# A two-stream diffusion layer on one core: VectorE's sums for a gate moved one transfer later and tied behind a subtraction

## The chip, the cores and the metric

The kernel runs on one core of a Trainium2 chip. The time is the device time of one execution in microseconds (us), the median of three runs. A profile is one execution more, with its own time; the trace is of that execution, and its span reaches from the first to the last instruction of the core.

## What is computed

One layer of a diffusion trunk is applied to two streams of 128 tokens with 2048 features: a context stream and a latent stream, which share all weights. Cut to what matters here:

```python
def adaln_params(cvec, w_ada_l, b_ada_l):
    mod = jax.nn.silu(cvec) @ w_ada_l + b_ada_l          # one vector per stream, 6 x 2048
    return jnp.split(mod[..., None, :], 6, axis=-1)      # sh1, sc1, g1, sh2, sc2, g2

h = modulate(rmsnorm(x, norm_mix_w), sh1, sc1) @ w_in    # 2048 x 8192
...                                                      # gated recurrence, short convolution, attention
x = x + g1 * (mixed @ w_out)                             # 2048 x 2048
h = modulate(rmsnorm(x, norm_ffn_w), sh2, sc2)
x = x + g2 * ((silu(h @ w_gate) * (h @ w_up)) @ w_down)  # hidden size 5632
```

The change touches the two gates, `g1` and `g2`: products of a vector per stream with a column block of `w_ada`, where the weights are read once and used for two vectors.

## The kernel before

**The stream of weights.** Every matrix is read in tiles of 512 rows by 512 columns (1 MB). `split` (line 238; `feature_mm`, line 289, does the same for weights that are held transposed) issues the tile's transfer on SyncE's queue, and then for each half of it ScalarE rounds the weights to the fp32r type (`hi`, line 253) and VectorE subtracts what was rounded from the weights (`lo`, line 254; line 299 in `feature_mm`). TensorE multiplies with both: per half tile eight matmuls with `hi` and four with `lo`, each of 512 columns, over two token streams (`products`, line 267). `hi` and `lo` have three buffers each, the raw tile four. In the last tiles of a matrix (`last_mm`) both halves have buffers of their own, and one token stream ends before the other.

**The modulation's weights.** There are 24 column blocks (chunks of 512 columns) of `w_ada`. The first eight are made ahead. Of the others, `LATER_T` (and chunk 20, in the pause behind `w_out`) go through TensorE (`later_pe`), and the seven chunks of `LATER_V`, 8 to 11 of `g1` and 21 to 23 of `g2`, through VectorE (`later_dve`, line 401): a chunk comes in eight parts, and each part is a GpSimd copy (line 411, which lets the transfer begin only when a recent tile is written), a transfer of 512 KB on GpSimd's queue (line 412) into one of two buffers `araw`, and four sums (line 415, `scalar_tensor_tensor`, 128x512 each) that add weights times the conditioning vector into `aacc`, of which there is one buffer. With the eighth part `later_gate` is started (lines 364 to 381): rounding on ScalarE (373), a subtraction (374), two matmuls that add over the partitions (379), and a copy out of PSUM (380), for each token stream.

**What sets the order.** The work is written down in an order made by hand. After each tile `behind` is called: it lets every started generator go on by one step (`pump`), and `ada_step` adds the phase's pace to two queues and takes parts from them when enough has come together. A part of a VectorE chunk costs 0.5; the pace of that queue is `PACE_V` = 0.19, 0.39, 0.08, 0.35 in the phases 0 to 3, which are the last round over the first seven column blocks of `w_in`, the other nine, `w_out`, and the feed-forward part without its first chunk. `gate(c)` (line 437) is called before a gate is used and takes whatever of it is still missing. The program is then put into an order for each engine by a planner: it plays the program through with a model of the durations and gives each engine, among the instructions that are ready in that model, the one with the best priority, which is its place in the program. Splits are raised by 600 places (`SPLIT_AHEAD`). On the chip each engine follows the order so made.

Of the kernel before, what the change touches and what calls it, by code (L numbers as in the profile page):

```python
# [10 lines left out]
F32 = mybir.dt.float32  # L11
# [4 lines left out]
ALU = mybir.AluOpType  # L16
# [76 lines left out]
def trunk(ctx: ExitStack, tc: tile.TileContext, a: dict):  # L93
    nc = tc.nc
    pool = ctx.enter_context(tc.tile_pool(name="sb", bufs=1))
    psum = ctx.enter_context(tc.tile_pool(name="ps", bufs=1, space=PSUM))
    uid = [0]
    ahead = [0]

    def sb(shape, tag, bufs, dt=F32):  # L100
        uid[0] += 1
        return pool.tile(shape, dt, tag=tag, name=f"{tag}_{uid[0]}", bufs=bufs)

    def const(shape, name, dt=F32):
        return pool.tile(shape, dt, tag=name, name=name, bufs=1)

    def u4(shape=(P, 2, CH)):
        return sb(list(shape), "u4", U4_BUFS)

    def u8(shape=(P, 2, 2, 4, P), dt=F32):  # L110
        return sb(list(shape), "u8", U8_BUFS, dt)

    def st(shape=(P, CH), dt=F32):
        return sb(list(shape), "st", ST_BUFS, dt)

    def aux(shape=(P, CH)):
        uid[0] += 1
        return psum.tile(list(shape), F32, tag="aux", name=f"aux_{uid[0]}", bufs=3)

    def accs():  # L120
        r = []
        for s in range(2):
            uid[0] += 1
            r.append(psum.tile([P, CH], F32, tag="acc", name=f"acc_{uid[0]}", bufs=4))
        return r
# [25 lines left out]
    cs = const([P, 16, 2], "cs")  # L151
# [76 lines left out]
    def spawn(gen):  # L228
        if next(gen, active) is not active:
            active.append(gen)  # L230

    def pump():
        for gen in list(active):
            if next(gen, active) is active:
                active.remove(gen)


    def split(src, apart=False):

        n = src.shape[1]  # L240
        with tc.high_priority(offset=ahead[0]):
            raw = sb([P, 4, CH], "raw", RAW_BUFS)
            nc.sync.dma_start(raw[:, 0:n], src)
            parts = []
            if apart:
                his, los = u8((P, 4, CH), F32R), u8((P, 4, CH), F32R)
            for j in range(n // 2):
                if apart:
                    hi, lo = his[:, 2 * j:2 * j + 2], los[:, 2 * j:2 * j + 2]
                else:  # L250
                    hi = sb([P, 2, CH], "hi", HL_BUFS, F32R)
                    lo = sb([P, 2, CH], "lo", HL_BUFS, F32R)
                nc.scalar.activation(hi, raw[:, 2 * j:2 * j + 2], AF.Copy)  # L253
                nc.vector.tensor_tensor(lo, raw[:, 2 * j:2 * j + 2], hi.bitcast(F32), op=ALU.subtract)  # L254
                parts.append((hi, lo))
        return parts

# [12 lines left out]
    def split_mm(src, acc, lhs, first, last, k0=0):  # L270

        parts = split(src)
        n = src.shape[1]
        for k in range(0, n, 2):
            products([(s, acc[s]) for s in range(2)], (k, k + 1), lhs, k0, parts, first and k == 0, last and k == n - 2)

    def last_mm(steps, acc, phase):

        tiles = []
        for src, lhs in steps:  # L280
            tiles.append((split(src, True), lhs))
            behind(phase)
        for s in range(2):
            for t, (parts, lhs) in enumerate(tiles):
                for k in (0, 2):
                    products([(s, acc[s])], (k, k + 1), lhs, 0, parts, False, t == len(tiles) - 1 and k == 2)
            yield s

    def feature_mm(src, rhs, accs2, first, last):

        with tc.high_priority(offset=ahead[0]):
            raw = sb([P, 8, 256], "raw", RAW_BUFS)
            nc.sync.dma_start(raw, src)
            parts = []
            for j in range(2):
                hi = sb([P, 4, 256], "hi", HL_BUFS, F32R)
                lo = sb([P, 4, 256], "lo", HL_BUFS, F32R)
                nc.scalar.activation(hi, raw[:, 4 * j:4 * j + 4], AF.Copy)  # L298
                nc.vector.tensor_tensor(lo, raw[:, 4 * j:4 * j + 4], hi.bitcast(F32), op=ALU.subtract)  # L299
                parts.append((hi, lo))  # L300
        for k in range(8):
            hi, lo = parts[k // 4]
            x = rhs(k)
            for b in range(2):
                ws = slice(b * P, (b + 1) * P)
                one = accs2[b][:, 0:256].rearrange("p (s t) -> p s t", s=2)
                for i, (w, y) in enumerate(((hi, x[0]), (hi, x[1]), (lo, x[0]))):
                    nc.tensor.matmul(one, lhsT=w[:, k % 4, ws], rhs=y, start=first and k == 0 and i == 0,  # L308
                                     stop=last and k == 7 and i == 2)
# [54 lines left out]
    def later_gate(c, parts, pe):  # L364

        yield
        yield
        g = u4()
        hl = None
        for s in range(2):  # L370
            if hl is None or not pe:
                hl = [st(dt=F32R), st(dt=F32R)]
                nc.scalar.activation(hl[0], parts[s], AF.Copy)
                nc.vector.tensor_tensor(hl[1], parts[s], hl[0].bitcast(F32), op=ALU.subtract)
                yield
                yield
            ps = aux()
            for i in range(2):
                nc.tensor.matmul(ps, lhsT=selb[:, s, :] if pe else ones, rhs=hl[i], start=i == 0, stop=i == 1)  # L379
            nc.scalar.activation(g[:, s, :], ps, AF.Copy)  # L380
        gates[c] = g
# [19 lines left out]
    def later_dve(c, part, box):  # L401

        if part == 0:
            box["acc"] = sb([P, 2, CH], "aacc", 1)
            nc.gpsimd.tensor_copy(box["acc"][:, :, 0:1], S["late"][:, :, 0:1])  # L405
            nc.gpsimd.memset(box["acc"], 0.0)
            for s in range(2):
                nc.gpsimd.dma_start(box["acc"][0:1, s, :], a["b_ada"][0:1, c * CH:(c + 1) * CH])
        acc = box["acc"]
        raw = sb([P, 2, CH], "araw", 2)  # L410
        nc.gpsimd.tensor_copy(raw[:, :, 0:1], S["late"][:, :, 0:1])  # L411
        nc.gpsimd.dma_start(raw, a["w_ada2"][c - 8, part // 2, :, 2 * (part % 2):2 * (part % 2) + 2, :])  # L412
        for k in range(2):
            for s in range(2):
                nc.vector.scalar_tensor_tensor(acc[:, s, :], raw[:, k, :], cs[:, 2 * part + k, s:s + 1], acc[:, s, :],  # L415
                                               op0=ALU.mult, op1=ALU.add)
        if part == 7:
            spawn(later_gate(c, [acc[:, 0, :], acc[:, 1, :]], False))

    queues = []  # L420
    boxes = {}
# [7 lines left out]
    def ada_step(phase):  # L429
        for queue, amount in zip(queues, (PACE_T[phase], PACE_V[phase])):  # L430
            queue[2] += amount
            while queue[0] and queue[2] >= queue[1] - 1e-6:
                queue[2] -= queue[1]
                fn, c, part, box = queue[0].pop(0)
                fn(c, part, box)

    def gate(c):
        while c not in gates:
            pump()
            for queue, _, _ in queues:  # L440
                if any(item[1] == c for item in queue):
                    fn, *args = queue.pop(0)
                    fn(*args)
        return gates[c]

    def behind(phase=None):

        pump()
        if phase is not None:
            ada_step(phase)  # L450
# [416 lines left out]
    part = {}  # L867
    for ri, (k0, nk) in enumerate(ROUNDS):
# [4 lines left out]
        for i, name in enumerate(ORDER[:START]):  # L873
            acc = accs()
# [15 lines left out]
    for name in ORDER[START:]:  # L890
        if name in FM:
            for half in range(2):
                acc = accs()
                for q in range(2):
                    feature_mm(a["w_infm"][2 * FM.index(name) + half, q],
                               lambda k: tuple(hT[2 * q + k // 4][:, :, x, k % 4, :] for x in range(2)), acc, q == 0, q == 1)
                    behind(1)
                for b in range(2):
                    consume_fm(name, 2 * half + b, acc[b][:, 0:256].rearrange("p (s t) -> p s t", s=2))
            continue  # L900
        acc = accs()
        for q in range(4):
            split_mm(w_in(q, name), acc, hT[q], q == 0, q == 3)
            behind(1)
        t = u4()
        for s in range(2):
            nc.scalar.activation(t[:, s, :], acc[s], AF.Copy)
        consume(name, t)
# [4 lines left out]
    for n in range(4):  # L913
        acc = accs()
# [28 lines left out]
    while queues[0][0] or active:  # L943
        ada_step(4)
        pump()
# [53 lines left out]
    for gi, grp in enumerate(groups):  # L999
# [6 lines left out]
        for n in range(4):  # L1006
            acc = accs()
# [113 lines left out]
```

## Time and profile before

| | us |
|---|---|
| median of three runs (1380.97, 1381.04, 1384.13) | 1381.04 |
| the profiled execution, its own time | 1374.68 |
| its span | 1372.9 |
| TensorE busy | 1338.6 |
| VectorE busy | 872.9 |
| ScalarE busy | 627.4 |
| GpSimd busy | 132.6 |

A TensorE that is busy is not one at its peak, since matmuls are pipelined and their ends are modelled. The distance from the start of one matmul to the start of the next tells more. Times of day below are counted from the start of the span.

### The profile page before, as it was taken

Reading aid. Unit: us, or ns where it says so; the run is one execution under the profiler, and the core shown is the slowest. Engines: PE = TensorE matmul, PEld = TensorE weight load, DVE = VectorE, ACT = ScalarE, POOL = GpSimd, SP = SyncE. Lnnn points to the kernel's source line nnn. Section 1 sums busy time; section 2 is a strip of 40 time slices with the busy share of each in tenths; the row PEclk is TensorE's granted clock in tenths of the full one; section 3 lists DMA queues with packets and bytes.
Section 4 is the critical chain, followed back from the end, with each engine's and each line's share of the span. In section 5 each row is a group of like instructions: output and inputs, shape, how many; then the busy total and the mean of one; then the engine's idle time right before and its main releaser. Section 6 shows DMA issues by size and latency. Waiting matters only on the chain. (4 is left out here: it accounts for less than half of the span.)

```text
span 1372.9 us, 19781 instructions
## 1 busy us (share of the span) xinstructions
PE 1338.6 (97%) x7936; PEld 1078.0 (79%) x7936; DVE 872.9 (64%) x1102; ACT 627.4 (46%) x839; POOL 132.6 (10%) x201
## 2 busy tenths in 40 slices
PE   5999999999999999999999999999999999999996
PEld 3667777797798897778788888888888888888885
DVE  3355558986977687477944888655555554455564
ACT  4433447655465443446444444444334444444442
POOL 0100001131222221001200222000000000000000
PEclk9999999999999999999999999999999999999998
DMA  8898976875787889865765677555555555555551
GB/s 349 304 357 305 343 296 220 306 289 200 290 303 254 312 313 357 311 262 192 268 227 187 219 271 245 214 184 189 203 201 207 190 192 197 184 184 186 204 193 62
DMA packets 54381, 335.39 MB, mean 244 GB/s; under 512 B 7249, under 2 KB 7313, under 8 KB 19217
## 3 DMA queue, kind: packets, MB, share of 16 engines
q1 hardware_dynamic: 42768, 296.79, 59.0%
q0 software_dynamic: 10944, 36.29, 7.6%
q8 instruction: 62, 1.02, 0.3%
q10 hardware_dynamic: 576, 1.05, 0.2%
q14 instruction: 31, 0.25, 0.0%
HBM read 330.43 MB, written 3.67 MB: 243 GB/s over the span
## 5 line engine op out<-in xcount | busy, mean ns | idle before, releaser
L267 PE MATMUL acc<-hi,u 128*128 128x512 f32 x2944 | 741.2, 393 | 2.0 <-ACT u L488 1.1
L254 DVE TENSOR_TENSOR lo<-raw,hi 128x1024 fp32r<-128x1024 f32 x368 | 448.6, 1223 | 346.5 <-ACT hi L253 339.2
L267 PEld LDWEIGHTS acc<-hi,u 128*128 128x128 f32 x2944 | 548.7, 188 | 138.1 <-issue 10.4
L253 ACT ACTIVATE hi<-raw 128x1024 fp32r<-128x1024 f32 x368 | 388.8, 1060 | 544.2 <-PE acc L267 426.7
L267 PE MATMUL acc<-lo,u 128*128 128x512 f32 x1472 | 397.1, 390 | 1.8 <-DVE lo L254 1.7
L267 PEld LDWEIGHTS acc<-lo,u 128*128 128x128 f32 x1472 | 275.5, 188 | 63.0 <-DVE lo L254 3.7
L415 DVE SCALAR_TENSOR_TENSOR aacc<-araw,cs,aacc 128x512 f32<-128x512 f32 x224 | 159.0, 746 | 42.9 <-DMA araw<-w_ada 38.8
L308 PE MATMUL acc<-u,hi 128*128 128x256 f32 x768 | 142.2, 286 | 0.0
L308 PEld LDWEIGHTS acc<-u,hi 128*128 128x128 f32 x768 | 119.2, 191 | 9.7 <-issue 5.0
L308 PE MATMUL acc<-u,lo 128*128 128x256 f32 x384 | 108.3, 286 | 0.0
L332 PE MATMUL ada<-raw,cst 128*32 128x256 f32 (+1 forms) x784 | 83.7, 484 | 11.3 <-DMA raw<-w_ada 11.3
L298 ACT ACTIVATE hi<-raw 128x1024 fp32r<-128x1024 f32 x48 | 50.9, 1059 | 63.7 <-PE acc L308 34.5
L308 PEld LDWEIGHTS acc<-u,lo 128*128 128x128 f32 x384 | 72.8, 191 | 5.0 <-issue 4.2
L411 POOL COPY araw<-u 128x2 f32<-128x2 f32 x56 | 51.4, 920 | 257.7 <-DVE aacc L415 195.6
L299 DVE TENSOR_TENSOR lo<-raw,hi 128x1024 fp32r<-128x1024 f32 x48 | 58.2, 1218 | 15.3 <-ACT hi L298 12.0
L332 PEld LDWEIGHTS ada<-raw,cst 128*32 128x32 f32 x784 | 23.8, 114 | 38.0 <-issue 27.7
L882 DVE TENSOR_TENSOR u<-u,acc 128x512 f32<-128x512 f32 x56 | 35.9, 682 | 25.0 <-PE acc L267 24.9
L412 POOL DMA_DIRECT2D araw<-w_ada x56 | 30.0, 536 | 15.0 <-POOL araw L411 14.4
L405 POOL COPY aacc<-u 128x2 f32<-128x2 f32 x7 | 3.2, 453 | 266.6 <-DVE u L882 163.6
L484 ACT ACTIVATE st<-aux,sh,sc 128x128 f32<-128x128 f32 x48 | 18.1, 455 | 12.8 <-DVE sc L353 10.6
L267 PE MATMUL acc<-u,u 128*128 128x512 f32 x96 | 22.1, 389 | 0.0
L267 PEld LDWEIGHTS acc<-u,u 128*128 128x128 f32 x96 | 18.0, 188 | 3.7
(218 smaller groups left out, 627.0 us busy)
## 6 DMA issues: line engine op xcount, KB each, us to landing
raw<-w_ada SPq DMA_DIRECT2D x66, 1024.0 KB, 7.1
raw<-w_gate SPq DMA_DIRECT2D x44, 1024.0 KB, 4.8
raw<-w_up SPq DMA_DIRECT2D x44, 1024.0 KB, 4.8
raw<-w_down SPq DMA_DIRECT2D x44, 1024.0 KB, 4.8
raw<-w_in SPq DMA_DIRECT2D x33, 1024.0 KB, 6.8
araw<-w_ada POOLq DMA_DIRECT2D x56, 512.0 KB, 5.9
raw<-w_infm SPq DMA_DIRECT2D x24, 1024.0 KB, 5.6
raw<-w_out SPq DMA_DIRECT2D x16, 1024.0 KB, 7.2
```

What stands on the lines that cost most here:

```text
L253: nc.scalar.activation(hi, raw[:, 2 * j:2 * j + 2], AF.Copy)
L254: nc.vector.tensor_tensor(lo, raw[:, 2 * j:2 * j + 2], hi.bitcast(F32), op=ALU.subtract)
L267: nc.tensor.matmul(acc, lhsT=lhs[:, s, x, k0 + k, :], rhs=w[:, k % 2, :], start=first and k == ks[0] and w is hi and x == 0, stop=last and ...
L298: nc.scalar.activation(hi, raw[:, 4 * j:4 * j + 4], AF.Copy)
L299: nc.vector.tensor_tensor(lo, raw[:, 4 * j:4 * j + 4], hi.bitcast(F32), op=ALU.subtract)
L308: nc.tensor.matmul(one, lhsT=w[:, k % 4, ws], rhs=y, start=first and k == 0 and i == 0, stop=last and k == 7 and i == 2)
L332: nc.tensor.matmul(box["acc"][32 * k:32 * k + 32, 0:cols.stop - cols.start], lhsT=cst[:, 4 * part + k, 2 - row:34 - row], rhs=raw[k // 2][ ...
L411: nc.gpsimd.tensor_copy(raw[:, :, 0:1], S["late"][:, :, 0:1])
L412: nc.gpsimd.dma_start(raw, a["w_ada2"][c - 8, part // 2, :, 2 * (part % 2):2 * (part % 2) + 2, :])
L415: nc.vector.scalar_tensor_tensor(acc[:, s, :], raw[:, k, :], cs[:, 2 * part + k, s:s + 1], acc[:, s, :], op0=ALU.mult, op1=ALU.add)
L484: nc.scalar.activation(h[:, s, j, :], ps[:, s, j, :], AF.Identity, bias=bias, scale=scale)
L882: nc.vector.tensor_tensor(part[name][:, s, :], part[name][:, s, :], acc[s], op=ALU.add)
```

## The change

The four sums of a part are no longer written down with the part's own transfer. They are put into a list, `waiting`, and written down by `flush`, which the next part calls right after its own transfer (and `gate` in its loop, and `ada_step` when the queue is empty). While they are written down, `issue_after` gives each of them an edge to the newest `lo` subtraction of the stream that has been written down by then: VectorE's order must have them behind it. The edge is one of order on the engine and no wait on a semaphore. With the eighth part `later_gate` is started from the same place.

```diff
                 nc.scalar.activation(hi, raw[:, 2 * j:2 * j + 2], AF.Copy)
-                nc.vector.tensor_tensor(lo, raw[:, 2 * j:2 * j + 2], hi.bitcast(F32), op=ALU.subtract)
+                newest[0] = nc.vector.tensor_tensor(lo, raw[:, 2 * j:2 * j + 2], hi.bitcast(F32), op=ALU.subtract)
...
         nc.gpsimd.dma_start(raw, a["w_ada2"][c - 8, part // 2, :, 2 * (part % 2):2 * (part % 2) + 2, :])
-        for k in range(2):
-            for s in range(2):
-                nc.vector.scalar_tensor_tensor(acc[:, s, :], raw[:, k, :], cs[:, 2 * part + k, s:s + 1], acc[:, s, :],
-                                               op0=ALU.mult, op1=ALU.add)
-        if part == 7:
-            spawn(later_gate(c, [acc[:, 0, :], acc[:, 1, :]], False))
+        def sums():
+            with tc.issue_after(newest[0].ins):
+                for k in range(2):
+                    for s in range(2):
+                        nc.vector.scalar_tensor_tensor(acc[:, s, :], raw[:, k, :], cs[:, 2 * part + k, s:s + 1],
+                                                       acc[:, s, :], op0=ALU.mult, op1=ALU.add)
+            if part == 7:
+                spawn(later_gate(c, [acc[:, 0, :], acc[:, 1, :]], False))
+
+        flush()
+        waiting.append(sums)
+
+    waiting = []
+
+    def flush():
+
+        while waiting:
+            waiting.pop(0)()
...
                 fn(c, part, box)
+        if not queues[1][0]:
+            flush()
...
                     fn, *args = queue.pop(0)
                     fn(*args)
+            flush()
         return gates[c]
```

The line in `feature_mm` is changed as the one in `split`.

## Rows read from the trace of the kernel before

**Rows 1.** The page, busy time and share of the span by engine.
```profile
PE 1338.6 (97%) x7936; PEld 1078.0 (79%) x7936; DVE 872.9 (64%) x1102; ACT 627.4 (46%) x839; POOL 132.6 (10%) x201
```

**Rows 2.** The chain that ended last, in order: start, length, what.
```profile
905.95 174.10 PE acc L267 x768
```

**Rows 3.** The sums by themselves: duration ns min/median/max, first and last start.
```profile
L415 DVE SCALAR_TENSOR_TENSOR aacc<-araw,cs,aacc x224: 716/746/758, 210.3 to 862.3; 128x512 f32<-128x512 f32 x112
```

**Rows 4.** Waits of PE, 200 to 870 us: us in total, times, longest.
```profile
PE acc L267 <- DVE lo L254: 1.7, 3, 0.7
PE ada L332 <- DMA raw<-w_ada: 1.0, 1, 1.0
PE aux L473 <- DVE st L486: 0.9, 1, 0.9
PE aux L456 <- DVE st L992: 0.6, 1, 0.6
```

**Rows 5.** Waits of VectorE, whole span, same columns.
```profile
DVE aacc L415 <- DMA araw<-w_ada: 38.8, 24, 5.5
```

**Rows 6.** Timeline of PE, 643 to 672 us: start, length, work, idle before.
```profile
645.12 1.97 PE L267 MATMUL acc<-hi,u 128*128 128x512 f32 x8
647.32 1.20 PE L267 MATMUL acc<-lo,u 128*128 128x512 f32 x4 [0.23 <-DVE lo L254]
...
660.18 1.98 PE L267 MATMUL acc<-hi,u 128*128 128x512 f32 x8
662.90 1.21 PE L267 MATMUL acc<-lo,u 128*128 128x512 f32 x4 [0.74 <-DVE lo L254]
663.95 2.01 PE L267 MATMUL acc<-hi,u 128*128 128x512 f32 x8
666.70 1.21 PE L267 MATMUL acc<-lo,u 128*128 128x512 f32 x4 [0.74 <-DVE lo L254]
667.75 2.01 PE L267 MATMUL acc<-hi,u 128*128 128x512 f32 x8
669.82 1.20 PE L267 MATMUL acc<-lo,u 128*128 128x512 f32 x4
```

**Rows 7.** Timeline of VectorE, the same stretch.
```profile
659.63 2.08 DVE L415 SCALAR_TENSOR_TENSOR aacc<-araw,cs,aacc 128x512 f32<-128x512 f32 x3 [1.14 <-DMA araw<-w_ada]
...
664.76 0.75 DVE L415 SCALAR_TENSOR_TENSOR aacc<-araw,cs,aacc 128x512 f32<-128x512 f32 x1 [1.25 <-DMA araw<-w_ada]
```

**Rows 8.** Timeline of VectorE, 835 to 865 us.
```profile
858.53 1.42 DVE L415 SCALAR_TENSOR_TENSOR aacc<-araw,cs,aacc 128x512 f32<-128x512 f32 x2 [0.63 <-DMA araw<-w_ada]
```

**Rows 9.** Lines 411 and 412 by themselves: duration ns min/median/max; the landings.
```profile
L411 POOL COPY araw<-u x56: 179/1062/4592, 204.0 to 851.4; 128x2 f32<-128x2 f32 x56
L412 POOL DMA_DIRECT2D araw<-w_ada x56: 527/530/569, 205.0 to 851.9; - x56
...
DMA to landing us min/median/max: 3.8/5.9/10.6
```

**Rows 10.** Timeline of VectorE at the end of w_out.
```profile
598.51 1.22 DVE L254 TENSOR_TENSOR lo<-raw,hi 128x1024 fp32r<-128x1024 f32 x1
...
604.35 2.98 DVE L415 SCALAR_TENSOR_TENSOR aacc<-araw,cs,aacc 128x512 f32<-128x512 f32 x4
608.74 0.69 DVE L927 TENSOR_TENSOR st<-acc,u 128x512 f32<-128x512 f32 x1 [1.42 <-PE acc L267]
...
610.88 1.22 DVE L254 TENSOR_TENSOR lo<-raw,hi 128x1024 fp32r<-128x1024 f32 x1 [0.72 <-ACT hi L253]
...
614.19 0.68 DVE L927 TENSOR_TENSOR st<-acc,u 128x512 f32<-128x512 f32 x1
```

**Rows 11.** Groups by form, whole span: busy us, mean ns, idle before.
```profile
L380 ACT ACTIVATE u<-aux 128x512 f32<-128x512 f32 x16 | 9.3, 586 | 3.4 <-PE aux L379 3.4
...
L373 ACT ACTIVATE st<-aacc 128x512 fp32r<-128x512 f32 x14 | 8.8, 627 | 15.9 <-DVE aacc L415 15.5 <-DVE st L374 0.3
```

**Rows 12.** Busy time by stretch: PE, PEld, DVE, ACT, POOL, clock, DMA, GB/s.
```profile
752.00:862.00 110.00, 109.36 (x494) 90.32 (x493) 93.31 (x113) 46.99 (x52) 26.63 (x36) 1.00 0.69 248
```

More of the change, by code (lines that the diff above doesn't have):

```diff
@@ L98, in trunk @@
     ahead = [0]
+    newest = [None]
     def sb(shape, tag, bufs, dt=F32):
@@ L298, in feature_mm @@
                 nc.scalar.activation(hi, raw[:, 4 * j:4 * j + 4], AF.Copy)
-                nc.vector.tensor_tensor(lo, raw[:, 4 * j:4 * j + 4], hi.bitcast(F32), op=ALU.subtract)
+                newest[0] = nc.vector.tensor_tensor(lo, raw[:, 4 * j:4 * j + 4], hi.bitcast(F32), op=ALU.subtract)
                 parts.append((hi, lo))
```

## Prediction

> **What bounds the kernel.** I read the page first: TensorE is busy for 1338.6 of 1372.9 us, VectorE for 64% of the span [rows 1]. The reader is to see that only what stops TensorE can change the time. The chain that ended last says what TensorE can do at best: 768 matmuls of line 267 in 174.10 us, 0.2267 us each [rows 2]; the sums run from 210 to 863 us [rows 3], and behind them the chain is almost nothing else, so the change has nothing to win there. What is left is the stretch from 200 to 870 us, and the table of TensorE's waits has four entries there: `lo` late (1.7), a modulation tile's transfer (1.0), the second norm's `L486` (0.9), and a transpose that waits for `L992` (0.6) [rows 4]. Against this VectorE waited 38.8 us, in 24 pieces, for the transfers of `araw` with a sum at the head of its queue [rows 5]. So most of that waiting is hidden behind TensorE's lead; the question is which pieces are not.
>
> The timeline of TensorE shows them. Eight `hi` matmuls take 8 x 0.2267 = 1.81 us, but four times the first `lo` matmul started later than that behind the first `hi` matmul [rows 6]: 647.32 - 645.12 = 2.20 (0.39 too much), 662.90 - 660.18 = 2.72 (0.91), 666.70 - 663.95 = 2.75 (0.94), 669.82 - 667.75 = 2.07 (0.26). Together 2.50 us. The idle times printed in these rows are smaller, since the ends of matmuls are modelled. VectorE's own timeline says why: a sum at 659.63 had waited 1.14 us for its transfer, one at 664.76 had waited 1.25, and the subtractions stood behind them in the queue [rows 7]. The fifth piece is at 860: between the two `L992` of a chunk two sums were placed that waited 0.63 us for their transfer [rows 8], and the transpose waited 0.6 for the second `L992` [rows 4].
>
> **The change, part by part.** It adds and removes no instruction: 224 sums, 56 copies, 56 transfers and seven `later_gate` stay, and SyncE's queue with the 1 MB tiles is not passed by anything. The edge is order alone, so what stands behind a sum on VectorE waits for the sum's 0.75 us [rows 3] as before. Three things move.
>
> First, the sums of part k are written down one part later, behind the newest `lo`. In the feed-forward part a tile is 24 matmuls, 5.44 us [rows 2], and at a pace of 0.35 against 0.5 a part comes every 1.43 tiles, 7.8 us. So a transfer gets 7.8 us more before a sum asks for it, and until then VectorE's queue holds `lo`s where it now holds waiting sums. The chunk without `ada_step`, to which the four pieces belong [rows 6], gets none of the sums that the planner now pulls forward into it. I take off the whole 2.50 us. At 860 I take off the 0.63 us of the transfer's wait. Sum: -3.13 us.
>
> Second, a buffer of `araw` is held one part longer, so the transfer of part k+2, in GpSimd's queue with the copy ahead of it, starts later. Sums k+2 are due two parts, 15.5 us, behind sums k; about 5 us of these I give to sums k themselves (four sums of 0.75 us and a subtraction or two of 1.22 among them [rows 3, 10]: an estimate). That leaves 10.5 us. The copy takes 1.06 us at the median, the issue 0.53, the landing 5.9 [rows 9], together 7.5, so 3 us are to spare, and this part costs 0. With the longest of all three (4.59, 0.57, 10.6) it would be 15.8 us, 5 late; that end goes into a rival.
>
> Here the row and a rule of the skill are weighed. The row shows copies of two elements per partition that take 0.18 us at the least and 4.59 at the most [rows 9]. The Trainium skill, "SBUF — State Buffer", section "Who interferes with whom", says that a VectorE instruction with two inputs in SBUF contends with a GpSimd instruction that reads SBUF, which the subtraction, the sum and the copy are. By that rule a VectorE that no longer pauses for transfers would shut the copy out for longer: if every copy took 4.59 us, the transfer would need 11.0 us, 0.5 more than there is; by the row's median it costs nothing. That VectorE is the one that loses is not to be seen: no sum took more than 758 ns, against 716 at the least [rows 3].
>
> Third, `later_gate` starts one part later, and with it the next chunk's `aacc`, which waits for the old one on GpSimd's queue; copies queued behind it wait too. For chunks 8 to 10 and 21 to 23 the gate is used tens of us later, so I cost this at nothing; the cover is that distance. Chunk 11 has the shortest. By the paces 7 x 0.19 + 36 x 0.39 = 15.37 is spent ahead of `w_out`; its eighth part, the 32nd of the queue, falls due at 16.0, with the eighth tile at 0.08 each, and the next part at 16.5 only with the fifteenth; so `gate(11)`, ahead of the last two tiles, writes the sums down. They must stand behind the `lo` of 598.51, the newest then, and four sums from 599.7 with 0.7 of other work end at about 603.4; then 0.63 (373), 0.69 (374, of the size of the `L927` in [rows 10]), two matmuls 0.45 [rows 2], 0.59 (380) [rows 11]: the first half of the gate is there at about 605.7, and its user starts at 608.74, the second half's at 614.19 [rows 10]. Three us of cover; cost 0. In return the four sums at 604.35 [rows 10], chunk 21's first, leave that place.
>
> VectorE is loaded more evenly, since the sums of `g2` spread over the chunks with `ada_step`, about 668 to 862 us. From 752 to 862 it was busy for 93.31 of 110 us, and TensorE was idle for only 0.64 [rows 12]; I take the same for the whole stretch: 0.
>
> The sum is -3.13 us. Against its own time, 1374.68, the profiled execution would become 1371.6; it lies 6.4 us under the median of the three runs, and I carry the difference over: 1381.04 - 3.13 = 1377.9 us.
>
> **The rivals.** *The waits stay.* The transfers are still late, by the copy's and the landing's longer ends, or the planner puts the sums as tightly as before. For it: the copies' spread [rows 9]. Against: 3 us to spare. With half of the pieces left it gives 1379.5, with all 1381.0.
>
> By the skill's rule on the shared interface alone the copies' 0.5 us on some 24 parts would be 12 us of waiting; at the ratio of 3.13 us lost to 38.8 waited that is 1 us, so 1378.9.
>
> *Small holes in a denser VectorE.* Now every chunk's end can have sums between its two `L992`. If each of the five chunks' ends got a hole like the largest, 0.94 us [rows 6], the cost is 4.7: 1381.0 - 3.1 + 4.7 = 1382.6. Against: the same mix from 752 to 862 had one hole.
>
> *Gate 11 comes too late* (the side of slower). The place is the end of `w_out`, where nothing but a short pause filled with modulation tiles covers the second norm. If the planner puts the four sums behind the subtraction of 610.88, they run from 612.0 to 615.0 and the gate's halves are there at 617.4 and 619.1, the second 4.9 us behind 614.19; the norm's own small operations, 2.1 us for the first token stream (612.1 to 614.2 [rows 10]), would then stand between, 7.0 in all. It decides from the point where the second half comes after 614.19, that is, with sums that end after about 611. Price 4.9 to 7.0, less 3.1 gained: 1382.8 to 1384.9, 1383.9 in the middle. Against: 3 us of cover.
>
> **How the numbers follow.** A difference of about 0.3%, 4.1 us, is what a measurement of this kernel can tell from no change. My forecast has 0.58, the waits that stay 0.18, the holes 0.13, gate 11 0.11. The forecast's own range is from 1375.9 (the waits for the modulation tile and for `L486`, 1.9 us [rows 4], fall away too, by new places) to 1379.5 (half of the pieces). The two rivals with losses reach to 1384.9; without the last half us, and with the three runs' own spread of 3.2 us in mind, I set 1375.5 to 1384.5. Faster by over 0.3% needs under 1376.9, which only the lower end of the forecast reaches: 0.16. Slower by over 0.3% needs more than 1385.2, gate 11 late at its worst or with holes besides: 0.10. The rest, 0.74, is within.
>
> **What would show it.** Right: VectorE's wait for `araw` falls from 38.8 us to a few, TensorE's wait for `lo` from 200 to 870 us is gone, no sum runs before 668 in the feed-forward part, and the chunks' last sum still ends near 862. Wrong: waits for `araw` that remain, a `L927` behind `L380` at the end of `w_out`, idle times at `L456` before each chunk's end, or a span shorter by more than 5 us, for which I have no place.

## The result and the profile after

The first comparison gave a median of 1373.38 us in four runs against 1381.01, a ratio of 0.9945 [0.9925, 0.9966]. That is 4.5 us under the forecast and 2.1 us under the range's lower end. The same two kernels, compared again in 10 and in 12 runs, gave 0.9977 [0.9961, 0.9993] and 0.9979 [0.9966, 0.9992], some 3 us. So the change makes the kernel faster, by the two larger comparisons by about 0.2%; why the first four pairs showed 7.6 us stays open, and what the runs say of it is told below.

The profiled execution took 1373.15 us. Its page, span and busy time, answers to [rows 1]:

```profile
span 1371.4 us, 19778 instructions
...
PE 1336.5 (97%) x7936; PEld 1078.0 (79%) x7936; DVE 872.4 (64%) x1102; ACT 627.2 (46%) x839; POOL 130.4 (10%) x201
```

Nothing in these sums tells where the time went: the same instructions took the same busy time, within 2.2 us on each engine. The waits of TensorE from 200 to 870 us (in total, times, longest) answer to [rows 4]:

```profile
PE aux L489 <- DVE st L502: 0.9, 1, 0.9
PE aux L346 <- DMA st<-b_ada: 0.6, 1, 0.6
PE ada L333 <- DMA raw<-w_ada: 0.6, 1, 0.6
PE aux L669 <- DVE u L676: 0.3, 1, 0.3
PE acc L268 <- DVE lo L255: 0.3, 1, 0.3
PE aux L656 <- DVE u L680: 0.2, 1, 0.2
```

The wait for `lo` fell from 1.7 to 0.3 us, and three entries are new: `b_ada`, and two steps of the recurrence (`L676`, `L680`). VectorE's own waits in the same stretch answer to [rows 5]:

```profile
DVE aacc L418 <- DMA araw<-w_ada: 25.9, 23, 3.0
DVE aacc L418 <- DMA aacc<-b_ada: 7.8, 4, 3.7
```

Two thirds of the 38.8 us of waiting for `araw` are still there. What is gone altogether is the waiting in the first feed-forward chunk, 8.5 us in four waits. Two of the four are in [rows 7]; the other two in VectorE's timeline of the kernel before are these:

```profile
644.05 2.08 DVE L415 SCALAR_TENSOR_TENSOR aacc<-araw,cs,aacc 128x512 f32<-128x512 f32 x3 [5.48 <-DMA araw<-w_ada]
...
653.49 1.42 DVE L415 SCALAR_TENSOR_TENSOR aacc<-araw,cs,aacc 128x512 f32<-128x512 f32 x2 [0.64 <-DMA araw<-w_ada]
```

Elsewhere the waiting only changed its place: before that chunk 20.6 us became 13.0, behind it 9.7 became 12.9. TensorE in the first feed-forward chunk of the changed kernel, against [rows 6]:

```profile
658.83 1.98 PE L268 MATMUL acc<-hi,u 128*128 128x512 f32 x8
660.65 1.07 PE L268 MATMUL acc<-lo,u 128*128 128x512 f32 x4
```

From the first `hi` matmul to the first `lo` matmul it is 660.65 - 658.83 = 1.82 us, the pure time of eight matmuls. And VectorE beside it, against [rows 7]:

```profile
664.66 1.23 DVE L255 TENSOR_TENSOR lo<-raw,hi 128x1024 fp32r<-128x1024 f32 x1 [1.49 <-ACT hi L254]
...
670.72 1.23 DVE L255 TENSOR_TENSOR lo<-raw,hi 128x1024 fp32r<-128x1024 f32 x1 [2.12 <-ACT hi L254]
671.87 0.75 DVE L418 SCALAR_TENSOR_TENSOR aacc<-araw,cs,aacc 128x512 f32<-128x512 f32 x1
```

No sum runs in this chunk before 671.87; each subtraction follows its `hi`.

**The time by stretch.** The cleanest reading takes the starts of matmuls from TensorE's timeline and subtracts them. On each engine the orders of all kernels here agree up to some 210 us, so the first mark is the 1270th matmul (228 to 234 us), shortly behind. The next are the last matmul of `w_in`'s transposed part (`feature_mm`), the first of the feed-forward part, the first of its second chunk and the first of its seventh; the sums are over by then. The stretch of `w_out` begins with that matrix's first matmul, 1.2 us behind the last of `feature_mm`. Behind the last mark every kernel takes 473.3 to 473.4 us. Each stretch holds the same matmuls in all kernels, but for e7, where eight short ones of the second norm fall into the first feed-forward chunk and not into the stretch ahead of it. The run's name is that of its experiment below.

| us | to 1270th | to the end of `w_in` | with `w_out` | first feed-forward chunk | second to sixth chunk | 1270th to the end |
|---|---|---|---|---|---|---|
| before | 227.99 | 288.22 | 105.82 | 50.35 | 225.89 | 1144.9 |
| before, e1 | 231.43 | 288.50 | 105.63 | 50.09 | 224.97 | 1143.8 |
| before, e12 | 234.40 | 291.77 | 105.63 | 50.75 | 225.43 | 1148.2 |
| after | 228.92 | 288.19 | 106.85 | 47.26 | 225.66 | 1142.5 |
| after, e2 | 231.67 | 288.99 | 107.41 | 47.27 | 224.93 | 1143.1 |
| after, e8 | 231.42 | 290.81 | 106.91 | 47.26 | 224.92 | 1144.4 |
| e3 move without tie | 230.25 | 303.96 | 109.51 | 50.84 | 224.92 | 1163.8 |
| e4 tie without move | 232.09 | 290.96 | 106.30 | 47.29 | 225.23 | 1144.4 |
| e10, as e4 | 233.12 | 288.43 | 105.99 | 47.27 | 225.79 | 1142.1 |
| e5 chunks 21 to 23 only | 227.56 | 288.92 | 105.89 | 47.26 | 224.92 | 1141.6 |
| e9, as e5 | 230.47 | 288.60 | 105.66 | 47.26 | 224.93 | 1141.1 |
| e11 as e5, tie alone | 229.58 | 289.36 | 105.63 | 47.27 | 226.15 | 1143.0 |
| e6 chunks 8 to 11 only | 229.07 | 291.70 | 107.08 | 50.62 | 225.30 | 1149.2 |
| e7 no wait for `araw` | 231.01 | 283.20 | 114.14 | 48.45 | 224.92 | 1145.3 |

Two columns tell the kernels apart in each of their three profiles: the first feed-forward chunk, 50.1 to 50.8 us before and 47.26 after (some 3.1 us gained), and `w_out`, 105.6 to 105.8 before and 106.9 to 107.4 after (1.0 to 1.8 lost). The other columns scatter as much within a kernel as between the two. How much one order scatters can be read off e4, e5, e9, e10 and e11, too: up to the end of `w_in` every engine of theirs has the order of the kernel before, and the eight profiles of that one order took 288.2 to 291.8 us there. In `w_out`, where TensorE's order is still the old one in them, the eight took 105.6 to 106.3.

### The profile page after: what moved, and what is told of

The parts are those of the page before. It is cut to its first block, busy times and chain, and to the rows that moved or that the text cites. A ratio compares the mean times of both kernels' runs of the same rounds, so it can differ in the third digit from the quotient of the medians.

```text
span 1371.4 us, 19778 instructions
## 1 busy us (share of the span) xinstructions
PE 1336.5 (97%) x7936; PEld 1078.0 (79%) x7936; DVE 872.4 (64%) x1102; ACT 627.2 (46%) x839; POOL 130.4 (10%) x201
## 3 DMA queue, kind: packets, MB, share of 16 engines
q10 hardware_dynamic: 576, 1.05, 0.2%
## 4 chain that ended last, share of the span: by engine, by line
PE 87%; DMA 7%; DVE 2%; issue 2%; ACT 1%; POOL 1%; SPq 0%; DVEq 0%; POOLq 0%; ACTq 0%
PE acc L268 71%; PE acc L309 7%; PE ada L333 5%; DMA araw<-w_ada 3%; DMA raw<-w_in 2%; DMA raw<-w_ada 1%; DVE aacc L418 1%; PE aux L472 1%; POOL araw L412 1%; DMA u<-xp 1%; DVE lo L255 0%; PE aux L489 0%; PE aux L380 0%; DMA st<-b_ada 0%; PE aux L646 0%
## 5 line engine op out<-in xcount | busy, mean ns | idle before, releaser
L418 DVE SCALAR_TENSOR_TENSOR aacc<-araw,cs,aacc 128x512 f32<-128x512 f32 x224 | 158.7, 746 | 33.8 <-DMA araw<-w_ada 25.9
L299 ACT ACTIVATE hi<-raw 128x1024 fp32r<-128x1024 f32 x48 | 50.8, 1059 | 54.0 <-PE acc L309 29.5
L898 DVE TENSOR_TENSOR u<-u,acc 128x512 f32<-128x512 f32 x56 | 36.0, 683 | 26.1 <-PE acc L268 25.9
```

The lines of the kernel that those rows point to most:

```text
L898: nc.vector.tensor_tensor(part[name][:, s, :], part[name][:, s, :], acc[s], op=ALU.add)
```

## The experiments

What had to be told apart: whether the order edge saves the four late `lo` pieces, by keeping the sums out of the first feed-forward chunk, or the part's delay, by giving the transfers time (the prediction's own reason); whether the waits as such are what costs, wherever they lie; and which of the two gates' chunks has what share. Ratios are to the kernel before, run beside it on the same chip.

**e1 and e2: both kernels once more.** No edit.

> The kernel before, unchanged, to see whether the 1381 us of its timed runs and the 1374.7 us of its profiled one are two kinds of executions of one program. Theory A (late transfers: the timed runs are those in which the transfers for the sums land later, and VectorE's queue then stops TensorE for longer): ratio to the kernel before 1.000, and a profile of an execution near 1381 us shows 8 to 10 us of TensorE waiting for the subtraction or for work behind it between 200 and 870 us, where the first profile had 3.1. Rival B (the difference lies elsewhere, for example in the first 200 us or in the start-up): the profile of an execution near 1381 us shows the same 3 us there and the other 6 us outside of that stretch.

> The changed kernel, unchanged. Both theories: 0.994 to 0.996 of the kernel before. Theory A: its executions lie within 1 us of 1373.4 whether the transfers are quick or late. Rival B: it has the same two kinds of executions as the kernel before, some 6 us apart.

The kernel before against itself gave 0.9999 [0.9985, 1.0013], 1379.44 us in 10 runs from 1377.03 to 1381.26. The changed one gave 0.9977 [0.9961, 0.9993], 1376.59 us against 1379.67. The gain is there, at less than half of the first measurement, and outside of what both theories expected; the ten runs reach from 1373.55 to 1378.58, so neither the 1 us of theory A nor two kinds of executions can be seen. The profiled execution of e1 took 1377.03 us, which is not near 1381 and could not answer its question; e12 comes back to it.

**e3: the move without the tie.** In the changed kernel:

```diff
-            with tc.issue_after(newest[0].ins):
+            if True:
```

> The sums are written down one part later, without the tie to the newest subtraction. Theory A1 (the lag alone gives the transfer its time): ratio 0.994 to 0.996, VectorE's wait for the transfers as small as in the changed kernel (26 us or less). Rival A2 (the planner pulls sums forward as before unless they are tied): ratio 0.998 to 1.000, VectorE's wait near 39 us.

It was slower, which neither theory had: 1.0139 [1.0116, 1.0162]. VectorE waited 43.5 us for `araw`, and the first feed-forward chunk kept its 50.84 us. A sum that is written down later still goes to the head of VectorE's queue ahead of its transfer. VectorE's timeline in this kernel:

```profile
378.75 2.74 DVE L418 SCALAR_TENSOR_TENSOR aacc<-araw,cs,aacc 128x512 f32<-128x512 f32 x4 [6.47 <-DMA araw<-w_ada]
381.41 0.68 DVE L680 TENSOR_TENSOR u<-u,T 128x512 f32<-128x512 f32 x1
382.01 1.22 DVE L676 TENSOR_TENSOR u<-u,T 128x1024 f32<-128x1024 f32 x1
```

TensorE's timeline at the same place:

```profile
383.28 0.48 PE L669 MATMUL aux<-u,u 128*64 128x64 f32 x2 [6.08 <-DVE u L676]
```

And two stretches (busy time of PE, PEld, DVE, ACT, POOL; granted clock, DMA share, GB/s):

```profile
380.00:385.00 5.00, 1.72 (x13) 1.27 (x15) 5.00 (x8) 0.00 (x0) 3.45 (x1) 0.65 0.00 0
385.00:390.00 5.00, 5.00 (x50) 4.88 (x48) 5.00 (x7) 3.08 (x5) 4.70 (x4) 0.66 0.78 228
```

Here a sum stood 6.47 us before the recurrence's `L680` and `L676`, for which TensorE waited 6.08 us; and from 380 to 390 us the granted clock was 0.65, so that TensorE, behind its idle time, ran for most of these stretches at 1.2 GHz and not at 2.4. The stretch to the end of `w_in` took 303.96 us, 12 to 16 more than in the three profiles of the kernel before. So the delay alone gives nothing and can cost much.

**e4 and e10: the tie without the move.** In the changed kernel the sums are tied and written down with their own transfer:

```diff
-        flush()
-        waiting.append(sums)
+        sums()
```

> The sums stay with their own transfer and are tied behind the newest subtraction. Theory A1: the transfer has no more time than before, ratio 0.998 to 1.002, VectorE's wait 39 us or more. Rival A2: the tie alone does it, ratio 0.994 to 0.997.

> The kernel of the run e4 once more (all chunks tied, none moved). Theory E (the tie is what removes the holes of the first feed-forward chunk, and the move by one part is what costs time in the first gate's chunks): 0.996 to 0.998, 47.3 us for the first feed-forward chunk and no wait of TensorE for L676, L680 or the b_ada transfer between 370 and 440 us. Rival F (the move is needed too): 0.999 to 1.001.

The first gave 0.9993 [0.9978, 1.0008], the second 0.9971 [0.9956, 0.9986], for one and the same kernel; so as timed this variant stays between no gain and 4 us. (The first one's median of ten runs, 1376.50 us, lay 3.2 us under the 1379.67 beside it, which its ratio doesn't show.) The first chunk took 47.29 and 47.27 us in the two: the tie alone takes the four pieces away, though VectorE still waited 28.2 and 29.8 us for `araw`.

**e5, e6, e9, e11: one gate at a time.** e5 and e9 (one kernel) move and tie only the chunks of `g2`, 21 to 23; e6 has `c < 12` in place of `c >= 12` and so only those of `g1`; e11 ties those of `g2` and moves none (`flush()` and then `sums()` for all). Against the changed kernel:

```diff
+        moved = c >= 12
+
         def sums():
-            with tc.issue_after(newest[0].ins):
+            with tc.issue_after(newest[0].ins) if moved else ExitStack():
...
         flush()
-        waiting.append(sums)
+        if moved:
+            waiting.append(sums)
+        else:
+            sums()
```

> Only the sums of the second gate's chunks (21 to 23) are moved and tied; chunks 8 to 11 stay as before. Theory A (the loss sat in the feed-forward part's first chunk, where sums waited ahead of subtractions): 0.997 to 0.998 of the kernel before, TensorE's waits between 640 and 700 us gone, those between 200 and 625 as before. Rival C (the gain comes from the first gate's chunks, between 200 and 600 us): 0.999 to 1.001.

> Only the sums of the first gate's chunks (8 to 11) are moved and tied; chunks 21 to 23 stay as before. Theory A: 0.999 to 1.001 of the kernel before, with 2 to 3 us of TensorE waiting for the subtraction between 640 and 700 us. Rival C: 0.994 to 0.997.

> The kernel of the run e5 once more (only chunks 21 to 23 moved and tied). If its lead over the whole change is real: 0.996 to 0.998 of the kernel before, 47.3 us for the first feed-forward chunk, and from the 231st us to the first feed-forward matmul about 395 to 396 us as in the kernel before. If it was chance: the ratio of the whole change, 0.998, and a similar number of holes between 370 and 490 us.

> Only chunks 21 to 23 are tied, and nothing is moved; the sums stand with their own transfer. Theory E: the same as e9, 0.996 to 0.998, with 47.3 us for the first feed-forward chunk. Rival F: first feed-forward chunk near 50 us and a ratio of 0.999 to 1.001.

Only `g2`: 0.9968 [0.9951, 0.9984] and again 0.9967 [0.995, 0.9984]; with the tie alone 0.9964 [0.995, 0.9978]. Only `g1`: 1.0009 [0.9993, 1.0024]. As far as these runs can tell, the whole gain is `g2`'s, and moving its sums adds nothing to tying them. All three are a little ahead of the whole change (0.9977, 0.9979), with intervals that overlap. In e6, without the tie on `g2`, VectorE's timeline shows the old picture:

```profile
643.15 1.23 DVE L255 TENSOR_TENSOR lo<-raw,hi 128x1024 fp32r<-128x1024 f32 x1 [0.25 <-ACT hi L254]
649.76 2.08 DVE L420 SCALAR_TENSOR_TENSOR aacc<-araw,cs,aacc 128x512 f32<-128x512 f32 x3 [5.38 <-DMA araw<-w_ada]
```

After one subtraction VectorE stood 5.38 us at a sum of chunk 21 that the planner had put there. In e11 VectorE's timeline holds only subtractions there, and the first sum comes at the end of the chunk:

```profile
642.59 1.23 DVE L255 TENSOR_TENSOR lo<-raw,hi 128x1024 fp32r<-128x1024 f32 x1 [1.49 <-ACT hi L254]
...
671.34 1.23 DVE L255 TENSOR_TENSOR lo<-raw,hi 128x1024 fp32r<-128x1024 f32 x1 [2.12 <-ACT hi L254]
672.48 2.07 DVE L420 SCALAR_TENSOR_TENSOR aacc<-araw,cs,aacc 128x512 f32<-128x512 f32 x3
```

This is the cleanest of the experiments. The subtraction at 642.59 is the first instruction in which any engine's order in e11 differs from the kernel before, which has the sum of 644.05 in its place; the other engines keep the old order to the end of the chunk. So nothing but this change of VectorE's order can have made the chunk 3.1 us shorter.

**e7: the waits taken away.** In the kernel before, the sums read the other half of `aacc` in place of the transferred weights, so nothing waits for `araw`; the products with the weights of the seven chunks are left out by this.

```diff
-                nc.vector.scalar_tensor_tensor(acc[:, s, :], raw[:, k, :], cs[:, 2 * part + k, s:s + 1], acc[:, s, :],
+                nc.vector.scalar_tensor_tensor(acc[:, s, :], acc[:, 1 - s, :], cs[:, 2 * part + k, s:s + 1], acc[:, s, :],
```

> The kernel before with sums that read the other half of their own accumulator in place of the transferred weights, so that no sum waits for a transfer; the transfers stay, and no result uses them. This leaves out the product with the weights of w_ada for the seven chunks. Theory A (the waits for transfers cost TensorE 2.5 to 3.1 us): 0.997 to 0.998. Rival B (in the usual execution the waits cost more than in the profiled one, 7 us or so): 0.994 to 0.996. Rival D (the waits cost nothing, the gain is from where the sums stand): 0.999 to 1.001.

All 38.8 us of waiting for `araw` were gone, and the time was the same: 0.9995 [0.9982, 1.0007]. That is theory D's number, but it is a sum of gains and losses that happened to cancel. Up to the end of `w_in` the run took 5 us less; 3.4 of them are the matmuls of the modulation tiles, which take 27.2 us there in the kernel before, in 29 groups, and 23.8 us here, in 26 (from the first start of each group to the start of the next other matmul). The first feed-forward chunk took 48.45 us with eight more short matmuls in it, and no `lo` in it came late: there the waits do cost what theory A says. `w_out` took 8 us more. Since these sums are ready as soon as they are written down, the planner filled the second norm with them. VectorE's timeline:

```profile
612.09 0.74 DVE L415 SCALAR_TENSOR_TENSOR aacc<-aacc,cs 128x512 f32<-128x512 f32 x1
612.75 0.15 DVE L202 TENSOR_SCALAR r_g<-r_v 128x1 int32<-128x1 int32 x1
```

TensorE's timeline behind it:

```profile
620.87 2.93 PE L473 MATMUL aux<-u,u 128*128 128x128 f32 x12 [4.11 <-DVE u L957]
624.89 5.02 PE L473 MATMUL aux<-u,u 128*128 128x128 f32 x20 [1.09 <-DVE u L957]
```

And two stretches, columns as in e3:

```profile
620.00:625.00 5.00, 3.04 (x13) 2.75 (x13) 5.00 (x14) 0.00 (x0) 0.00 (x0) 0.50 0.53 223
625.00:630.00 5.00, 4.95 (x21) 4.68 (x22) 4.93 (x10) 3.46 (x8) 0.00 (x0) 0.50 0.01 2
```

A chain of small operations of 0.15 us each is stretched by sums of 0.74 us between them, TensorE waits 4.11 and then 1.09 us for its end, and the granted clock is 0.50 (1.2 GHz) from 620 to 630 us. So the run gives no clean price for all the waits, since it changed the order elsewhere. That most of the waiting costs TensorE nothing is shown by e4, e10 and e11: 28.2 to 30.9 us of it are left in them, and the four late pieces are gone.

**e8: the changed kernel a third time.** No edit.

> The changed kernel, unchanged, once more, on the chip of these runs. Theory A: 0.997 to 0.998, the -3 us of the sum worked out ahead. Rival B: 0.994 to 0.996, as in the first four pairs of runs.

It gave 0.9979 [0.9966, 0.9992], 1376.82 us in 12 runs. Its profile shows the dearest of the new holes. TensorE's timeline:

```profile
430.06 0.28 PE L309 MATMUL acc<-u,lo 128*128 128x256 f32 x1
431.49 1.03 PE L346 MATMUL aux<-sel,st 128*128 128x4 f32 x8 [1.15 <-DMA st<-b_ada]
```

GpSimd's timeline:

```profile
419.70 0.53 POOL L413 DMA_DIRECT2D araw<-w_ada  x1 [0.30 <-POOL araw L412]
...
424.34 1.03 POOL L399 DMA_DIRECT2D st<-b_ada  x2
438.58 0.19 POOL L406 COPY aacc<-u 128x2 f32<-128x2 f32 x1 [13.21 <-DVE st L375]
```

The stretch, columns as in e3:

```profile
430.00:435.00 5.00, 3.85 (x26) 3.67 (x26) 2.57 (x5) 1.76 (x4) 0.00 (x0) 0.80 0.98 408
```

The transfer of a bias (`st<-b_ada`, line 399), issued on GpSimd's queue at 424.34, landed only for 431.49, TensorE stood 1.15 us, and the stretch had a granted clock of 0.80. The wait is 0.6 in the first profile of the changed kernel, 1.6 in e3, 0.2 in e6, and absent from the list in e2 and wherever the chunks of `g1` stay in their place (before, e1, e4, e5, e9 to e12).

**e12: the kernel before a third time**, to see what one execution's luck is worth. No edit.

> The kernel before, unchanged, to see how far two executions of one program differ behind the place where the orders of the kernels part (the 1270th matmul, at 228 to 233 us). If the stretches are the kernel's own, the first feed-forward chunk takes 50.1 to 50.4 us again, w_out 105.6 to 105.8, the stretch ahead of it 288.2 to 288.5 and the second to sixth chunk 225 to 226, so that the changed kernel's 47.26 and its 106.9 are its own. If they are one execution's luck, the first chunk falls under 48.5 or w_out rises above 106.5. Time: ratio 1.000 within 0.0015.

0.9994 [0.9979, 1.001]; `w_out` took 105.63 us, as expected, and the first chunk 50.75, a little over the 50.4 and far from the changed kernel's 47.26. The stretch ahead of `w_out` took 291.77 and not 288.2 to 288.5, so that one is not the kernel's own. The profiled execution was a long one, 1384.38 us, and the table says where: 6.4 us more than the first profile of the same program up to the 1270th matmul and 3.6 more up to the end of `w_in`. For e1 this speaks in the main for rival B: the late `lo`s cost TensorE hardly more in a long execution (2.1 us of its waits, against 1.7 in [rows 4]), and two thirds of the difference lie ahead of the stretch in question. TensorE's timeline:

```profile
279.24 1.41 PE L332 MATMUL ada<-raw,cst 128*32 128x512 f32 x8 [1.89 <-DMA raw<-w_ada]
```

The stretch behind it, columns as in e3:

```profile
280.00:285.00 5.00, 5.00 (x31) 4.42 (x28) 2.96 (x4) 2.22 (x5) 1.98 (x4) 0.68 0.75 272
```

The wait for a modulation tile that was 1.0 us in [rows 4] was 1.89 here, and the clock behind it fell to 0.68 of full in that stretch.

## Why the prediction was wrong, point by point

**The first term, four late pieces, was right in place and nearly in size.** -2.50 us was forecast; the first chunk went from between 50.1 and 50.8 us to 47.26, about -3.1. Nearly all of what the forecast lacked can be read off the timeline of [rows 6]: behind each late start the group of four `lo` matmuls took 1.03 to 1.05 us to the next start (663.95 - 662.90 = 1.05) in place of 4 x 0.2267 = 0.91, in all four some 0.5 us that the forecast left out. The reason put first was wrong: "a transfer gets 7.8 us more before a sum asks for it" describes the move, and the move does nothing here (e3 keeps 50.84; e11 without it has 47.27). The remark behind it was the cause, that the chunk "gets none of the sums that the planner now pulls forward into it", and it is the tie that does this: the chunk takes 47.3 us in every kernel whose `g2` sums are tied, and 50.1 to 50.8 in every other in which the sums wait for the transfers. As a sign of success "VectorE's wait for `araw` falls from 38.8 us to a few" was wrong with the reason: 25.9 us remain. Of the other signs, no sum ran before 668 us in the feed-forward part (the first at 671.87), the wait for `lo` fell to 0.3 us and not to nothing, and the last sum started at 865.7 us, later than the 862 named.

**The hole at 860** was to bring 0.63 us. In the changed kernel's profile another one stands near its place. VectorE's timeline, against [rows 8]:

```profile
861.41 0.75 DVE L418 SCALAR_TENSOR_TENSOR aacc<-araw,cs,aacc 128x512 f32<-128x512 f32 x1 [3.00 <-DMA araw<-w_ada]
862.08 1.22 DVE L255 TENSOR_TENSOR lo<-raw,hi 128x1024 fp32r<-128x1024 f32 x1
```

TensorE's timeline:

```profile
861.05 1.97 PE L268 MATMUL acc<-hi,u 128*128 128x512 f32 x8
863.35 1.20 PE L268 MATMUL acc<-lo,u 128*128 128x512 f32 x4 [0.32 <-DVE lo L255]
```

863.35 - 861.05 = 2.30, 0.49 more than the 1.81 of eight matmuls. The second to sixth chunk took 224.9 us, with no such hole, in e2 and e8, but 225.0 in e1, the kernel before; e11 has one of 0.96 us at 860. So the holes here come and go within one kernel, and the term should not have been counted.

**Gate 11 in time: right.** VectorE's timeline at the end of `w_out`, against [rows 10]:

```profile
598.85 1.41 DVE L418 SCALAR_TENSOR_TENSOR aacc<-araw,cs,aacc 128x512 f32<-128x512 f32 x2
...
600.31 1.40 DVE L418 SCALAR_TENSOR_TENSOR aacc<-araw,cs,aacc 128x512 f32<-128x512 f32 x2
...
601.79 1.36 DVE L375 TENSOR_TENSOR st<-aacc,st 128x512 fp32r<-128x512 f32 x2
...
610.73 0.69 DVE L943 TENSOR_TENSOR st<-acc,u 128x512 f32<-128x512 f32 x1 [0.60 <-issue]
```

ScalarE's timeline:

```profile
608.60 1.07 ACT L381 ACTIVATE u<-aux 128x512 f32<-128x512 f32 x2
```

The sums stand behind the last subtraction of the matrix, as worked out (599.7 forecast, 598.85 measured). The gate's two halves are there at about 609.2 and at 608.60 + 1.07 = 609.67, later than the 605.7 forecast for the first; their users start at 610.73 and 616.12. There was some 1.5 us of cover where three were reckoned, but it held.

**The chunks of `g1` at no cost: this step failed.** "I cost this at nothing" looked only at the distance to the gate's use. But a new order is a new order of everything. In `w_out` the planner now broke one modulation tile's eight matmuls in two. TensorE's timeline in the changed kernel:

```profile
528.53 1.04 PE L333 MATMUL ada<-raw,cst 128*32 128x512 f32 x2
529.51 1.20 PE L268 MATMUL acc<-lo,u 128*128 128x512 f32 x4
530.63 1.06 PE L333 MATMUL ada<-raw,cst 128*32 128x512 f32 x6
531.62 2.09 PE L268 MATMUL acc<-hi,u 128*128 128x512 f32 x8
```

and in the kernel before:

```profile
528.53 1.07 PE L332 MATMUL ada<-raw,cst 128*32 128x512 f32 x8
529.53 2.12 PE L267 MATMUL acc<-hi,u 128*128 128x512 f32 x8
```

From start to start the two take 0.98 us and the six 0.99, the eight together 1.00; between these matmuls a group costs that with two, six or eight in it, so breaking it costs 1.0 us. A tile of `w_out`'s stretch is broken so in each profile in which `g1`'s chunks are moved (after, e2, e3, e6, e8) and in none of the kernel before and of e4, e5, e9, e10 and e11. So among these it is the move that does it; e7, which moves nothing but has another order too, breaks one as well. Second, the recurrence got the small holes for `L676`, `L680` and `b_ada` named above (e3 in the extreme). Both are losses that e5 doesn't have. The 1.0 us in `w_out` stands in every such profile; what the holes cost scatters too much to be read off the table, and the timed difference between the whole change and e5, some thousandth, is within the intervals.

**The buffer held longer, and the rule on the shared interface.** Cost 0 was forecast, and between e5 and e11, which differ in the move alone, none is seen. The sums by themselves (ns min/median/max), against [rows 3]:

```profile
L418 DVE SCALAR_TENSOR_TENSOR aacc<-araw,cs,aacc x224: 721/746/754, 220.1 to 865.7; 128x512 f32<-128x512 f32 x112
```

GpSimd's copies by themselves, against [rows 9]:

```profile
L412 POOL COPY araw<-u x56: 183/1115/3731, 204.9 to 850.7; 128x2 f32<-128x2 f32 x56
```

The copies' median rose by 0.05 us and the longest fell from 4.59 to 3.73, so VectorE's denser work did not shut them out, and the rule alone would not have brought the sum to 1378.9. The Trainium skill, "SBUF — State Buffer", section "Who interferes with whom", has GpSimd and VectorE contend there; the trace fits that on GpSimd's side, where a copy of two elements took up to 3.73 us (what made it long is not shown), and shows hardly a loss on VectorE's, where no sum took over 754 ns.

**The step that put the result outside the range** was "it lies 6.4 us under the median of the three runs, and I carry the difference over". Against its own execution the sum was -3.13 us, and the two large comparisons gave about -3.2 and -2.9 by their ratios; behind the 1270th matmul the three profiles of each kernel differ by 1143.3 - 1145.6 = -2.3 in the mean. But the 6.4 us are no constant of the kernel. The changed kernel's profiled execution lay 0.2 us under the median of its four. So of the 7.66 us between the medians 1381.04 and 1373.38 only 1.53 lie between the two profiled executions (1374.68 and 1373.15); the other 6.13 are the offset that was carried over and did not come. e12 shows such an offset in one program: 6.4 us of it lie ahead of the 1270th matmul. What made all four runs before fall at 1380.6 to 1384.1 and all four after at 1373.2 to 1376.6 is open: there is no profile of the kernel before at 1381 from that chip. The changed kernel's other 22 runs, on two other occasions, reach from 1373.55 to 1379.48, and three of its first four lie under the fastest of these; the 25, 35 and 26 runs of the kernel before beside the other experiments have medians of 1379.2 to 1380.4, so its own was near theirs. If the 26 runs of the changed kernel were alike, its three fastest would all fall among a given four about once in 650 times (an estimate by counting). So a lucky draw is an unlikely account, and a state of that chip in which the changed kernel ran faster is not shown either.

Of the rivals, gate 11 and holes at each chunk's end didn't come; the waits stay was right about the waits and wrong about their worth. The chance of 0.74 stood on a difference within 0.3%; the large comparisons say 0.2%, the first one 0.55%.

**The best version** is e11's or e5's, only the chunks of `g2` tied, 0.9964 to 0.9968: it keeps the 3.1 us of the first chunk and gives nothing back in `w_out`. That it beats the whole change is likely by the stretches, but within the intervals of the times. A larger gain may lie untouched: between the 1270th matmul and the end of `w_in` the kernel before breaks six of its 22 modulation tiles as well, which by 1.0 us a tile is some 5 us (27.2 against 22, an estimate; no run tried it).

## What to carry to other kernels

Where a planner orders an engine's queue, what a wait costs is decided by what is queued behind it: find the few waits that have the bottleneck's next operand behind them and move only those, with an edge of order, rather than shift all the work in time. A local edge can replan everything else, so cut the timeline at fixed matmuls and compare all the stretches, not only the one that was meant. And forecast a difference between like executions, with the spread of the runs as the range, before adding the distance of one profile to a median of three.

## What was not expected of the hardware

- One program on one core scattered by 10 to 14 us: 25 runs of the kernel before on one chip reached from 1373.49 to 1387.36. The mean granted clock goes with it: the five of them at 0.992 had a mean of 1382.7 us, the eight at 0.994 one of 1378.2, the one at 0.996 took 1374.6. In the profiles the differences lie mostly where all kernels have the same order, in the first 230 us (227.6 to 234.4).
- A hole of 1 to 2 us on TensorE can cost more than itself. Behind 1.03 us of waiting for the modulation tile the stretch had a clock of 1.00 (kernel before, 275 to 280 us), and so it had behind 1.62 us (e11, 275 to 280); behind 1.89 us it was 0.68 (e12) and behind 2.05 us 0.88 (e4, 280 to 285). But with 1.15 us of waiting for a bias at 431 us the stretch from 430 to 435 had 0.80 (e8). So the length of a hole alone didn't tell whether it was dear.
- A group of matmuls with a 32-column stationary tile took 0.97 to 1.00 us from start to start with two, six or eight of them, between other matmuls of 256 and 512 columns; one of sixteen took 1.85 (changed kernel, 422.9 us).
